# Contrast adjustment on one core: three of seven stores moved to ScalarE's queue, the last tile clipped and stored in halves

## The chip, the core and the metric

The kernel runs on one core of one Trainium2 chip. The metric is the device time of one execution in microseconds (us); before the change the median of three runs is 239.53 us (239.49 to 239.54). The core has five instruction streams that matter here: PE (TensorE), DVE (VectorE), ACT (ScalarE), POOL (GpSimd) and SP (SyncE). Each runs its own instructions in order. Transfers between device memory and the on-chip memory (128 partitions) are issued by one of these streams and then moved by the core's 16 DMA engines.

## What is computed

The input is a batch of 16 images with 3 planes of 512 x 512 float32 numbers, 50.33 MB. Each plane's contrast is stretched about its own mean, and the result is clipped to 0..1:

```python
def reference(x, factor):                      # x: 16 x 3 x 512 x 512, factor = 1.5
    mean = np.mean(x, axis=(2, 3), keepdims=True)
    return np.clip(mean + factor * (x - mean), 0, 1).astype(np.float32)
```

In other words out = clip(factor * x + (1 - factor) * mean, 0, 1). A plane's mean has to be known before any of its numbers can be written, so each number is loaded once, kept on chip, and stored once: 50.33 MB in and 50.33 MB out.

## The kernel before

A plane's 262144 numbers are cut into 16 rows of 16384, one row per partition. So one tile of 128 partitions x 16384 columns (8.39 MB) holds eight planes, and the 48 planes make six tiles, numbered 0 to 5. On chip there is one buffer named `ring` with three slots (BUFS = 3); tile t lies in slot t % 3. Tiles 3, 4 and 5 can be loaded only when the stores of tiles 0, 1 and 2 have left their slots. Slots, columns and waits are worked out by the framework from what each instruction reads and writes; the order of the instructions on each stream is the order in which the program is written (manual_schedule).

The steps of one tile:

- The load (line 77), issued by SP. Tile 0 comes in three pieces: columns 0 to 2047, 2048 to 8191, and 8192 to 16383. The others come in one.
- The row sums (function `add`). DVE sums the first 4352 columns (line 85), ACT the other 12032 with a copy onto themselves that also accumulates (line 89). For tile 0 this is done once for each half of the columns, with 4352 and 3840.
- The shift. PE multiplies the row sums by a block matrix whose entries are (1 - factor)/262144 inside each plane's 16 partitions (line 100), which leaves (1 - factor) * mean on each partition, in `bias`.
- The clip, two passes of DVE in place: multiply and add (line 103), then max with 0 and min with 1 (line 106). For tile 0 it is done in two column parts, 2048 and 14336 columns wide; here their stores are called 0a and 0b.
- The store (line 80), issued by SP, one for each part that is clipped.

The order in which SP issues is: the three pieces of load 0, loads 1 and 2, stores 0a, 0b, 1 and 2, loads 3, 4 and 5, stores 3, 4 and 5. So SP issues load 3 only after it has issued store 2, and that waits for the clip of tile 2. ACT issues no transfers. DVE's order is, tile after tile, its sum and then the two passes of the clip.

Of the kernel before, what the change touches and what calls it, by code (L numbers as in the profile page):

```python
# [1 line left out]

# [4 lines left out]


P = 128  # L10
ROW = 16384
HALF = ROW // 2
BUFS = 3
SHORT = 2048
SUM = 4352


@with_exitstack
def kernel(
    ctx: ExitStack,  # L20
    tc: tile.TileContext,
    x: bass.AP,
    factor: float,
    out: bass.AP,
):

    nc = tc.nc
    f32 = mybir.dt.float32  # L30
    Alu = mybir.AluOpType
    Act = mybir.ActivationFunctionType

    B, C, H, W = x.shape
    n_img, n_pix = B * C, H * W
    ppi = n_pix // ROW
    per_tile = P // ppi
    n_tiles = n_img // per_tile
    assert ppi * ROW == n_pix and per_tile * n_tiles == n_img

    factor = float(factor)
    wconst = (1.0 - factor) / float(n_pix)

    x_f = x.rearrange("b c h w -> (b c h w)")
    out_f = out.rearrange("b c h w -> (b c h w)")

    def dram(ap, t, c0=0, c1=ROW):
        return bass.AP(tensor=ap.tensor, offset=t * P * ROW + c0, ap=[[ROW, P], [1, c1 - c0]])

    consts = ctx.enter_context(tc.tile_pool(name="consts", bufs=1))  # L50
    xpool = ctx.enter_context(tc.tile_pool(name="xpool", bufs=1))
    small = ctx.enter_context(tc.tile_pool(name="small", bufs=1))
    psum = ctx.enter_context(tc.tile_pool(name="psum", bufs=1, space=bass.MemoryType.PSUM))


    sums = small.tile([P, 4 * n_tiles], f32, name="sums")
    bias = psum.tile([P, n_tiles], f32, name="bias")

    blockw = consts.tile([P, P], f32, name="blockw")
    blocks = blockw.rearrange("p (a b) -> p a b", b=ppi)  # L60
    nc.gpsimd.memset(blockw, wconst)  # L61
    for base, step in ((0, -ppi), (ppi - 1, ppi)):
        nc.gpsimd.affine_select(  # L63
            out=blocks,
            in_=blocks,
            compare_op=Alu.is_ge,
            fill=0.0,
            base=base,
            pattern=[[step, per_tile], [0, ppi]],
            channel_multiplier=1 if step < 0 else -1,  # L70
        )


    ring = xpool.tile([P, BUFS, ROW], f32, name="ring")

    def load(t, c0=0, c1=ROW):
        nc.sync.dma_start(out=ring[:, t % BUFS, c0:c1], in_=dram(x_f, t, c0, c1))  # L77

    def store(t, c0=0, c1=ROW):
        nc.sync.dma_start(out=dram(out_f, t, c0, c1), in_=ring[:, t % BUFS, c0:c1])  # L80

    def add(t, col, c0, c1, c2):
        xt = ring[:, t % BUFS, :]
        own = sums[:, 4 * t + col : 4 * t + col + 2]
        nc.vector.tensor_reduce(  # L85
            out=own[:, 0:1], in_=xt[:, c0:c1], axis=mybir.AxisListType.X, op=Alu.add
        )
        part = xt[:, c1:c2]
        nc.scalar.activation(out=part, in_=part, func=Act.Copy, accum_out=own[:, 1:2])  # L89
        return [own[:, 1:2], own[:, 0:1]]  # L90

    def compute(t, *cuts):
        xt = ring[:, t % BUFS, :]
        if t == 0:
            parts = add(t, 0, 0, SUM, HALF) + add(t, 2, HALF, HALF + SUM, ROW)
        else:
            parts = add(t, 0, 0, SUM, ROW)
        shift = bias[:, t : t + 1]
        for k, part in enumerate(parts):
            nc.tensor.matmul(shift, blockw, part, start=k == 0, stop=k == len(parts) - 1)  # L100
        for c0, c1 in zip((0, *cuts), (*cuts, ROW)):
            part = xt[:, c0:c1]
            nc.vector.tensor_scalar(  # L103
                out=part, in0=part, scalar1=factor, scalar2=shift, op0=Alu.mult, op1=Alu.add
            )
            nc.vector.tensor_scalar(  # L106
                out=part, in0=part, scalar1=0.0, scalar2=1.0, op0=Alu.max, op1=Alu.min
            )
            store(t, c0, c1)

    with tc.manual_schedule():
        load(0, 0, SHORT)
        load(0, SHORT, HALF)
        load(0, HALF, ROW)
        load(1)
        load(2)
        compute(0, SHORT)
        compute(1)
        compute(2)
        load(3)  # L120
        load(4)
        load(5)
        compute(3)
        compute(4)
        compute(5)


# [1 line left out]
_INS = ['x', 'factor']  # L129
_OUTS = [((16, 3, 512, 512), 'float32')]  # L130

_NUMBERS = {'factor': 1.5}


# [26 lines left out]
```

## Time and profile before

| what | value |
|---|---|
| median of three runs | 239.53 us |
| span of the profiled execution, first to last instruction | 237.3 us |
| moved by DMA | 100.66 MB, mean 424 GB/s over the span |
| DVE busy | 137.4 us, 58% of the span |
| ACT busy | 59.9 us, 25% |
| PE busy | 7.9 us, 3% |
| one clip pass of a whole tile (line 103, line 106) | 8.76 us, 8.70 us |
| ACT's sum of 12032 columns | 10.23 us |
| DVE's sum of 4352 columns | 4.68 us |

The profile is of one execution whose span is given; the time measured for a run is longer than the span by what lies before the first and behind the last instruction (2.2 us, taken against the median of the runs; the profiled execution's own total isn't given apart from its span). All times in the views count from the first instruction. A line such as "L103 DVE" is what line 103 of the kernel let DVE do. "SPq" is the instruction with which SP issues a transfer, and its time isn't that of the transfer. Where rows are merged ("x4"), the time runs from the first one's start to the last one's end. In brackets stands how long the engine was idle before, and what ended that. Rates in short stretches count a packet where it starts, so they jump by whole packets.

### The profile page before, as it was taken

The numbers are of one execution on the slowest core, as the hardware profiler recorded it, in microseconds if no ns is written. First come the engines' busy times: TensorE is split into PE (matmuls) and PEld (weight loads), VectorE is DVE, ScalarE is ACT, GpSimd is POOL, SyncE is SP. The second block draws the span as 40 slices with busy tenths as digits, with TensorE's granted clock in tenths as the row PEclk, the third lists the DMA queues.
The fourth block names the chain that finished last, engine by engine and source line by source line (L and its number), as shares of the span: only waits on it lengthen the run. The fifth ranks groups of instructions, "written<-read, shape, count | busy, mean of one in ns | idle before, by whom it ended". The sixth has DMA issues, their size and how long they took to land.

```text
span 237.3 us, 186 instructions
## 1 busy us (share of the span) xinstructions
PE 7.9 (3%) x28; PEld 6.9 (3%) x28; DVE 137.4 (58%) x21; ACT 59.9 (25%) x15; POOL 1.1 (0%) x7
## 2 busy tenths in 40 slices
PE   0010100010001000000000000100000000000000
PEld 0010100010001000000000000100000000000000
DVE  0071899949998998000000043499989998991000
ACT  2051300980492000000000049319509800000000
POOL 1000000000000000000000000000000000000000
DMA  7999989899799798989899998989899998989894
GB/s 289 418 442 442 530 353 530 353 486 398 331 464 454 341 530 353 530 353 519 365 442 442 398 486 353 530 354 530 353 475 409 431 453 376 508 353 530 353 530 177
DMA packets 2160, 100.66 MB, mean 424 GB/s; under 512 B 240, under 2 KB 240, under 8 KB 240
## 3 DMA queue, kind: packets, MB, share of 16 engines
q1 hardware_dynamic: 2160, 100.66, 98.7%
HBM read 50.33 MB, written 50.33 MB: 424 GB/s over the span
## 4 chain that ended last, share of the span: by engine, by line
DVE 43%; DMA 36%; ACT 9%; PE 2%; SPq 1%; issue 0%; DVEq 0%; ACTq 0%
DMA ring<-in_x_dram 36%; DVE ring L103 18%; DVE ring L106 18%; ACT ring L89 9%; DVE sums L85 6%; PE bias L100 2%; SPq L77 1%; SPq L80 0%; DVEq L103 0%; ACTq L89 0%
## 5 line engine op out<-in xcount | busy, mean ns | idle before, releaser
L89 ACT ACTIVATE ring<-ring 128x12032 f32<-128x12032 f32 (+1 forms) x7 | 58.0, 8280 | 128.2 <-DMA ring<-in_x_dram 128.2
L85 DVE TENSOR_REDUCE sums<-ring 128x1 f32<-128x4352 f32 x7 | 32.8, 4683 | 63.9 <-DMA ring<-in_x_dram 63.9
L103 DVE TENSOR_SCALAR ring<-ring,bias 128x16384 f32<-128x16384 f32 (+2 forms) x7 | 52.8, 7538 | 12.9 <-PE bias L100 12.9
L106 DVE TENSOR_SCALAR ring<-ring 128x16384 f32<-128x16384 f32 (+2 forms) x7 | 52.3, 7476 | 0.2
L100 PE MATMUL bias<-sums,blockw 128*128 128x1 f32 x28 | 7.9, 360 | 189.1 <-ACT ring L89 175.4
L100 PEld LDWEIGHTS bias<-sums,blockw 128*128 128x128 f32 x28 | 6.9, 314 | 190.0 <-ACT ring L89 159.4
L89 ACT ACT_TABLE_LOAD x1 | 1.3, 1283 | 0.8 <-PEq L142 0.8
L89 ACT ACTIVATION_READ_ACCUMULATOR ring<-ring 128x1 f32 x7 | 1.3, 187 | 0.0
L63 POOL TENSOR_SCALAR_AFFINE_SELECT blockw<-blockw 128x128 f32<-128x128 f32 x2 | 0.7, 340 | 0.1
L61 POOL MEMSET blockw<- 128x128 f32 x1 | 0.2, 204 | 0.3 <-POOLq L142 0.3
L142 POOL MEMSET const-bfloat16-1.0<- 128x1 bf16 x1 | 0.1, 102 | 0.0
L142 POOL MEMSET const-uint8-127<- 128x1 uint8 x1 | 0.1, 102 | 0.0
L142 POOL MEMSET const-float32-0.0<- 128x1 f32 x1 | 0.1, 98 | 0.3 <-issue 0.3
L142 POOL MEMSET const-float32-1.0<- 128x1 f32 x1 | 0.1, 98 | 0.0
## 6 DMA issues: line engine op xcount, KB each, us to landing
out_dram<-ring SPq DMA_DIRECT2D x1, 7168.0 KB, 35.9
ring<-in_x_dram SPq DMA_DIRECT2D x1, 4096.0 KB, 20.8
ring<-in_x_dram SPq DMA_DIRECT2D x1, 3072.0 KB, 11.6
ring<-in_x_dram SPq DMA_DIRECT2D x1, 1024.0 KB, 4.7
out_dram<-ring SPq DMA_DIRECT2D x1, 1024.0 KB, 34.3
ring<-in_x_dram SPq DMA_DIRECT2D x5, 57.7
out_dram<-ring SPq DMA_DIRECT2D x5, 27.0
```

What stands on the lines that cost most here:

```text
L61: nc.gpsimd.memset(blockw, wconst)
L63: nc.gpsimd.affine_select(out=blocks, in_=blocks, compare_op=Alu.is_ge, fill=0.0, base=base, pattern=[[step, per_tile], [0, ppi]], channel ...
L77: nc.sync.dma_start(out=ring[:, t % BUFS, c0:c1], in_=dram(x_f, t, c0, c1))
L85: nc.vector.tensor_reduce(out=own[:, 0:1], in_=xt[:, c0:c1], axis=mybir.AxisListType.X, op=Alu.add)
L89: nc.scalar.activation(out=part, in_=part, func=Act.Copy, accum_out=own[:, 1:2])
L100: nc.tensor.matmul(shift, blockw, part, start=k == 0, stop=k == len(parts) - 1)
L103: nc.vector.tensor_scalar(out=part, in0=part, scalar1=factor, scalar2=shift, op0=Alu.mult, op1=Alu.add)
L106: nc.vector.tensor_scalar(out=part, in0=part, scalar1=0.0, scalar2=1.0, op0=Alu.max, op1=Alu.min)
L142: nc = _bacc.Bacc("TRN2", target_bir_lowering=False, num_devices=1)
```

## The change

Stores of tiles whose slot is 0, that is 0 and 3, are issued by ACT instead of SP; the others stay on SP. `compute` is split in two functions, `total` (the row sums) and `clip` (matmuls, the two passes, and the store), called in the same order as before for the first five tiles. Three things differ besides. The store of tile 3 is not issued from its clip but after the row sums of tile 4 have been put down, so on ACT it stands behind the sum of tile 4 and ahead of the sum of tile 5. On ACT the stores 0a and 0b stand behind the two sums of tile 0 and ahead of the sum of tile 1. And tile 5 is clipped in two halves of 8192 columns, each stored on its own (here 5a and 5b).

```diff
     def store(t, c0=0, c1=ROW):
-        nc.sync.dma_start(out=dram(out_f, t, c0, c1), in_=ring[:, t % BUFS, c0:c1])
+        queue = nc.scalar if t % BUFS == 0 else nc.sync
+        queue.dma_start(out=dram(out_f, t, c0, c1), in_=ring[:, t % BUFS, c0:c1])
...
-    def compute(t, *cuts):
+    parts = {}
+
+    def total(t):
+        if t == 0:
+            parts[t] = add(t, 0, 0, SUM, HALF) + add(t, 2, HALF, HALF + SUM, ROW)
+        else:
+            parts[t] = add(t, 0, 0, SUM, ROW)
+
+    def clip(t, *cuts):
         xt = ring[:, t % BUFS, :]
...
-            store(t, c0, c1)
+            if t != BUFS:
+                store(t, c0, c1)
...
-        compute(0, SHORT)
-        compute(1)
-        compute(2)
+        total(0)
+        clip(0, SHORT)
+        total(1)
+        clip(1)
+        total(2)
+        clip(2)
         load(3)
         load(4)
         load(5)
-        compute(3)
-        compute(4)
-        compute(5)
+        total(3)
+        clip(3)
+        total(4)
+        store(3)
+        clip(4)
+        total(5)
+        clip(5, HALF)
```

On SP's queue this leaves: loads 0 (three pieces), 1 and 2, stores 1 and 2, loads 3, 4 and 5, stores 4, 5a and 5b.

More of the change, by code (lines that the diff above doesn't have):

```diff
@@ L90, in add @@
         return [own[:, 1:2], own[:, 0:1]]
-    def compute(t, *cuts):
+    parts = {}
[5 more added lines that the diff above has]
+    def clip(t, *cuts):
         xt = ring[:, t % BUFS, :]
[L94 to L97, printed above, removed]
         shift = bias[:, t : t + 1]
-        for k, part in enumerate(parts):
-            nc.tensor.matmul(shift, blockw, part, start=k == 0, stop=k == len(parts) - 1)
+        for k, part in enumerate(parts[t]):
+            nc.tensor.matmul(shift, blockw, part, start=k == 0, stop=k == len(parts[t]) - 1)
         for c0, c1 in zip((0, *cuts), (*cuts, ROW)):
```

## The prediction

> **What bounds the kernel now.** I read the page's DMA rows first, then the chain of waits, then a table of stretches cut where one transfer follows another, and last the timeline of each engine.
>
> ```profile
> DMA packets 2160, 100.66 MB, mean 424 GB/s; under 512 B 240, under 2 KB 240, under 8 KB 240
> q1 hardware_dynamic: 2160, 100.66, 98.7%
> DVE 43%; DMA 36%; ACT 9%; PE 2%; SPq 1%; issue 0%; DVEq 0%; ACTq 0%
> ```
>
> One queue kept the 16 DMA engines busy for 98.7% of the span. The chain names DVE for 43%, but it follows whatever released a transfer last; the next table says that the transfers themselves leave no room. Its columns: stretch, length, busy time of the engines, granted clock, DMA share, GB/s.
>
> ```profile
> 0.80:1.80 1.00, 0.00 (x0) 0.00 (x0) 0.00 (x0) 1.00 (x1) 0.86 (x3) 1.00 0.00 0
> ...
> 57.90:60.30 2.40, 0.00 (x0) 0.00 (x0) 2.40 (x1) 0.00 (x0) 0.00 (x0) 1.00 1.47 437
> 60.30:61.40 1.10, 0.00 (x0) 0.00 (x0) 1.10 (x1) 0.00 (x0) 0.00 (x0) 1.00 0.00 0
> ```
>
> The same table, one transfer a line:
>
> ```profile
> 41.50:62.00 20.50, 1.01 (x4) 0.93 (x4) 17.43 (x3) 10.32 (x2) 0.00 (x0) 1.00 0.90 367
> ...
> 81.40:100.70 19.30, 0.00 (x0) 0.00 (x0) 12.31 (x2) 0.00 (x0) 0.00 (x0) 1.00 0.99 431
> 100.70:120.10 19.40, 0.00 (x0) 0.00 (x0) 0.00 (x0) 0.00 (x0) 0.00 (x0) 1.00 1.01 436
> ...
> 178.10:197.50 19.40, 1.18 (x4) 1.00 (x4) 18.61 (x4) 10.32 (x2) 0.00 (x0) 1.00 1.01 439
> 197.50:216.80 19.30, 0.00 (x0) 0.00 (x0) 17.03 (x2) 0.00 (x0) 0.00 (x0) 1.00 1.00 435
> ```
>
> Whole tiles of 8.39 MB follow each other every 19.4 us, loads and stores alike. Only load 2 took 20.5: for 1.1 us after 60.3 no new row began. Twelve tiles at 19.36 make 232.3 us; with 1.1 for that stall, 1.2 at the end (no row after 236.1 of 237.3) and the 2.7 left over for the start (first issue at 0.80, no packet before 1.80, a slow first microsecond), that is the span. So nothing but the stall can be gained, and the question is whether the change leaves the DMA engines without work.
>
> The timeline: SP's issues of stores 0a to 2 merged, then tile 1's sum and clip and tile 2's sum.
>
> ```profile
> 30.52 63.63 SPq L80 DMA_DIRECT2D out_dram<-ring  x4
> 41.93 10.23 ACT L89 ACTIVATE ring<-ring 128x12032 f32<-128x12032 f32 x1 [15.86 <-DMA ring<-in_x_dram]
> 53.43 8.76 DVE L103 TENSOR_SCALAR ring<-ring,bias 128x16384 f32<-128x16384 f32 x1 [3.07 <-PE bias L100]
> 62.22 8.70 DVE L106 TENSOR_SCALAR ring<-ring 128x16384 f32<-128x16384 f32 x1
> 62.40 10.23 ACT L89 ACTIVATE ring<-ring 128x12032 f32<-128x12032 f32 x1 [10.15 <-DMA ring<-in_x_dram]
> ```
>
> The timeline again, SP alone: load 4.
>
> ```profile
> 101.08 0.34 SPq L77 DMA_DIRECT2D ring<-in_x_dram  x1
> ```
>
> ACT's starts give the landings of loads 1 and 2 (41.93, 62.40); load 4 is issued at 101.08, when store 1 has landed. A landing shows some 0.4 us after the slowest engine goes on to its next row, so the engines finish store 1 at 100.7. Store 2, issued at 93.82, is waiting there by then: a reserve of 100.7 - (93.82 + 1.0) = 5.9 us, with the 1.0 from issue to first packet at the start.
>
> The packet count gives the size of a piece: 15 transfers x 16 engines x 9 = 2160, eight partition rows and one small entry (the 240) per engine and transfer. A full row (64 KB) takes 19.4/8 = 2.42 us; a row of store 0a (2048 columns, 8 KB) 0.30; a row of store 0b (14336 columns) 2.12. Store 0a is 2.42 in all, store 0b 16.9.
>
> **The change part by part.** The profiled span of 237.3 lies 2.2 below the median of 239.53, which I add as a constant.
>
> 1. *Stores 0a and 0b on ACT.* Now both stand in SP's queue behind loads 1 and 2 and move nothing before 61.4. On a second queue they can move from 31.5 (issue 30.52 + 1.0) and 46.8, and delay the loads by what they put between. The trace has one queue only, so how the engines share is unknown. Bounds for load 2's delay: none (rows stay behind the loads), or 2.42 + 16.5 = 18.9 (equal shares by bytes from 46.8 on, where load 2 has 16.5 of work left and store 0b 16.9). I take alternation row by row, because the packets of the trace are rows: bursts of one row on each of the 16 engines every 2.42 us. Load 1's rows change at 22.2 + 2.42k (load 0 landed at 22.58, less 0.4), so the first 8 KB row goes in at 31.9, after its row 4; one follows each load row, and the eighth comes after row 3 of load 2. Store 0b, long issued, then goes in after rows 4 to 7: four rows, or three if the engine had already taken its next row at 31.9. Load 2 is delayed by 2.42 + 4 x 2.12 = 10.9 and lands at 73.3 (71.2 with three).
>
> 2. *ACT's order.* The issue of 0b waits for the second clip pass of tile 0 (45.76), and ACT's sum of tile 1 is queued behind it: it starts at 46.2 instead of 41.93 (load 1 lands at 43.2 to 44.4, so that is hidden in the same wait). From the start of ACT's sum to the clip is 53.43 - 41.93 = 11.50; both passes take 8.77 + 0.02 + 8.70 = 17.49. Clip 1 ends at 75.2 instead of 70.9 and store 1 can move at 76.2; the engines have loads and store 0 until 81.4, which hides it with 5.2 to spare. DVE's sum of tile 2 follows until 79.9.
>
> 3. *Store 2 and what stands behind it.* ACT's sum of tile 2 starts at 73.3, its clip at 84.8 (DVE is free at 79.9, and 0.7 for the matmuls makes 80.6, so ACT ends last), store 2 is issued at 84.8 + 17.49 + 0.07 = 102.4 and moves at 103.4. SP is in order: loads 3, 4 and 5 are behind that issue, although their slots are free (store 0 done before 90, store 1 at 101.1). The engines run dry at 100.7: **a gap of 2.7 us**, passed on whole to everything later, since the rest is back to back. With three rows it is 0.6. The point from which it costs anything is load 2 landing at 100.7 - 1.0 - 29.1 = 70.6.
>
> 4. *Restart and mixing.* After a gap the first rows are slow: the first microsecond of data at the start moved at 213 GB/s against 418 in the next, half a microsecond lost; a store needn't repeat it, so 0 to 0.5, taken as 0. Switching between load and store rows: load 5, followed by a store, landed 178.57 - 159.21 = 19.36 after load 4, no loss; load 2, followed by the small rows of 0a, lost 1.1. So for each of some 15 switches between nothing and 1.1, at most 8 of them with small rows (+8.8), and at best the old stall goes (-1.1). I take no change.
>
> 5. *Store 3 on ACT, issued after ACT's sum of tile 4.* Times of before, to be shifted by the gap: that sum ends at 169.5, clip 3 at 168.9, so ACT doesn't wait, and the issue (0.34) is over long before load 5 lands. Store 3 moves from 170.6 beside load 5, which has three rows left; alternation (or equal bytes) delays load 5 by 7.3, to 185.9. ACT's sum, then clip 5 at 185.9 + 11.5 = 197.4, against 197.08 now, where DVE ends last: 0.3 later. The total of work is unchanged, and store 4 (191.8) is there before store 3 is through at 197.5. Nothing on the path; if the store went wholly first, load 5 would land at 197.9, and the first half of store 5 would move at 219.4 against 216.8, a gap of 2.6.
>
> 6. *The last tile in halves.* Passes of 8192 columns by the line through the rows for 2048 and 14336 (1.29 and 7.69; 1.23 and 7.63): 4.49 + 4.43 = 8.92 a half, 17.84 for both, 0.4 more than now. Half 5a is issued near 206.4, half 5b near 215.3; 5a's 9.7 us of rows cover 5b behind store 4's end at 216.8. Store 5 is already there at 214.64 + 1.0, so the earlier start gains nothing. Rows half as long cost nothing that load 0c (4 MB: 22.55 - 12.86 = 9.7) doesn't show.
>
> 7. *Issues.* SP has three fewer and one more, ACT three more, 0.34 each, all beside waits. POOL and PE are untouched.
>
> Sum: 2.7 + 0 + 0 = +2.7, so 239.5 + 2.7 = **242.2**; this case alone runs from 239.0 (three rows, the stall gone: 0.6 - 1.1) to 243.3 (a slow restart and a little mixing).
>
> The Trainium skill, DMA: Bandwidth & Descriptors, section Queues, rings and completion order, says that an engine goes round its queues by packets and drains one of about 9 to 17 descriptors before it switches. If the nine entries of a transfer on an engine are one such packet, the second rival below holds and the sum would be 0; no run here shows yet which unit it is.
>
> **The rivals.** *Equal shares by bytes.* Store 0a takes its 1 MB at half rate by 36.3, 0b and load 2 end nearly together: load 2 lands at 62.4 + 18.9 = 81.3, store 2 is issued at 110.4, and the gap is 10.7 (9.6 net if the stall goes): 249.1 to 250.2. For it: equal competitors. Against: the trace moves whole rows one after another on an engine.
>
> *Whole transfers in turn* (or one order for both queues). Load 2 lands no later than 62.4 + 2.4 = 64.9, tile 2's clip waits for DVE (80.6), store 2 is issued at 98.1 and moves at 99.1, before 100.7. No gap: 239.5; the placement on two queues then does nothing. This is also where it ends on the other side: if 0a's small rows no longer stand behind load 2's last row and that 1.1 us stall goes with them, 238.4. It decides as long as load 2 lands by 70.6. For it: nine entries a transfer. Against: nothing in the trace marks the nine as one unit.
>
> *Stores first, or costly mixing.* Priority of stores gives 10.7 and the 2.6 of step 5: 252.8; mixing at 1.1 on each of eight small rows adds up to 8.8 to the sum: 251.
>
> **How the numbers follow.** Rows in turn 0.52, equal bytes 0.20, whole transfers 0.18, stores first or costly mixing 0.10. A change under 0.2% (0.48 us) can't be told from none here. Slower: 0.46 of the first, all of the second and the last: 0.76. Same: 0.04 + 0.12 = 0.16. Faster: 0.02 + 0.06 = 0.08. The range reaches from 238.6 to 250.2, leaving out the lucky end of whole transfers and most of the last case.
>
> **What would show it.** Two queues in the DMA rows; ACT's sum of tile 1 at 46.2 and of tile 2 at 71 to 73 (65: whole transfers; 80 or more: equal bytes); SP issuing store 2 at 100 to 102 and loads right behind it; a hole in GB/s just after 100; later tiles shifted by the same few microseconds; no hole after 200. It is wrong if load 2 lands before 70.6, or if rows of 64 KB take clearly over 2.42 us while both queues move.

## The result and the profile after

The changed kernel takes 243.37 us (243.29 to 244.03) against 239.51 (239.11 to 239.54) beside it: 1.0167 times the time, 95% interval 1.0155 to 1.0179, or 3.9 us slower. The forecast was 242.2 in a range of 238.6 to 250.2. The profiled execution took 243.29 with a span of 241.5, so 1.8 us lie around the span; spans compared, the change cost 4.2.

The page of the changed kernel, its DMA rows:

```profile
DMA packets 2304, 100.66 MB, mean 417 GB/s; under 512 B 256, under 2 KB 256, under 8 KB 256
q1 hardware_dynamic: 1872, 83.89, 81.6%
q10 hardware_dynamic: 432, 16.78, 16.1%
```

There are two queues now, and together they fill 97.7% of the engines' span where one filled 98.7%. The bytes are the same; the time that the engines were without work, or slow, has grown. The table of stretches shows where (columns as before: stretch, length, engines, clock, DMA share, GB/s):

```profile
81.20:100.50 19.30, 1.01 (x4) 0.93 (x4) 15.92 (x2) 2.17 (x2) 0.00 (x0) 1.00 0.97 422
100.50:102.90 2.40, 0.00 (x0) 0.00 (x0) 1.53 (x1) 0.00 (x0) 0.00 (x0) 1.00 0.00 0
102.90:119.90 17.00, 0.00 (x0) 0.00 (x0) 0.00 (x0) 0.00 (x0) 0.00 (x0) 1.00 1.00 432
```

From 100.5 to 102.9 no row was moved: a hole of 2.4 us, counted from the last engine's end to the first one's start (2.6 on the mean of the 16 engines). What it waited for stands in the timeline; these are the lines of ACT and DVE on tiles 1 and 2 and of SP behind them:

```profile
46.14 10.23 ACT L90 ACTIVATE ring<-ring 128x12032 f32<-128x12032 f32 x1 [20.16 <-DVE ring L111]
73.05 10.23 ACT L90 ACTIVATE ring<-ring 128x12032 f32<-128x12032 f32 x1 [16.58 <-DMA ring<-in_x_dram]
84.54 8.76 DVE L108 TENSOR_SCALAR ring<-ring,bias 128x16384 f32<-128x16384 f32 x1 [4.82 <-PE bias L105]
102.09 0.34 SPq L81 DMA_DIRECT2D out_dram<-ring  x1
102.61 21.60 SPq L77 DMA_DIRECT2D ring<-in_x_dram  x3
```

In the kernel before, the clip of tile 2 and the issue of store 2 are these lines:

```profile
76.26 8.76 DVE L103 TENSOR_SCALAR ring<-ring,bias 128x16384 f32<-128x16384 f32 x1 [0.75 <-PE bias L100]
93.82 0.33 SPq L80 DMA_DIRECT2D out_dram<-ring  x1
```

ACT's sum of tile 1 started at 46.14, let go by DVE and no longer by the load, since the issue of store 0b stands ahead of it. Load 2 landed at 73.05 instead of 62.40, the clip of tile 2 started at 84.54 instead of 76.26, and SP issued store 2 at 102.09 instead of 93.82. Only then came load 3, although nothing else held it.

The hole isn't all. DVE's sum of tile 3 and ACT's sum of tile 4 start at 143.25 and 162.66, later by 3.5 than before (139.79 and 159.21), and the span ends 4.2 later. The missing parts are longer stretches in which no row was started, at two places where loads and stores meet. The same table, first of the changed kernel (store 2's last row, and the row of load 5 before store 3 comes in):

```profile
120.10:122.85 2.75, 0.00 (x0) 0.00 (x0) 0.00 (x0) 0.00 (x0) 0.00 (x0) 1.00 0.00 0
174.25:176.85 2.60, 0.00 (x0) 0.00 (x0) 2.56 (x1) 0.00 (x0) 0.00 (x0) 1.00 0.00 0
```

and of the kernel before, just behind the end of its store 2, and in load 5's last row:

```profile
120.10:121.80 1.70, 0.00 (x0) 0.00 (x0) 0.00 (x0) 0.00 (x0) 0.00 (x0) 1.00 0.00 0
175.65:177.45 1.80, 0.00 (x0) 0.00 (x0) 1.80 (x1) 0.00 (x0) 0.00 (x0) 1.00 0.00 0
```

A row takes 2.42 us. In the kernel before the engines start theirs over some 0.6, so 1.7 to 1.8 us without a start is the rhythm of undisturbed engines. In the changed kernel they start within 0.15 and 0.35 of each other at these places, which would leave 2.3 and 2.1; 2.75 and 2.6 is more. The packets of the trace settle it: averaged over the 16 engines, the row at 120 lasted 0.73 too long and the one at 174 0.81, where the kernel before has 0.0 and 0.1. I call these pauses.

Load 2's delay can be read in the trace too. Two stretches of the changed kernel, with the packets and MB of each queue (q1 is SP's, q10 ACT's); first 42.8 to 53.7 us, load 2's first four rows beside store 0a:

```profile
q1 hardware_dynamic: 71, 4.19, 88.8%
q10 hardware_dynamic: 64, 0.52, 11.3%
```

4.19 MB are 64 full rows, 0.52 MB are 64 rows of 8 KB: each of 16 engines took four of each in turn, and the queues' bytes stand eight to one. (The 7 others on q1 are completion entries, the small entries at a transfer's end.) And 68.6 to 72.7 us, the end of load 2 beside store 0b, with the rates in 40 slices of 0.1 us:

```profile
GB/s 0 0 0 0 0 0 0 0 0 0 0 0 0 0 0 0 1119 3357 1678 2797 0 0 0 0 0 0 0 0 0 0 0 0 0 0 0 0 559 559 3357 3916
q10 hardware_dynamic: 31, 1.78, 100.0%
q1 hardware_dynamic: 16, 0.00, 0.2%
```

SP's queue moves nothing more than 16 entries of a few bytes, one per engine: the completion entries of load 2. The packets show its last data row ending at 70.55 on the slowest engine. Ten of the entries follow by 70.64, but six engines reach theirs only at 72.4 to 72.7, behind one more row of store 0b. ACT sees the load at 73.05, 2.5 us after the last data row, where some 0.4 is usual.

### The profile page after: what moved, and what is told of

It is laid out like the page before. It is cut to its first block, busy times and chain, and to the rows that moved or that the text cites. A ratio compares the mean times of both kernels' runs of the same rounds, so it can differ in the third digit from the quotient of the medians.

```text
span 241.5 us, 188 instructions
## 1 busy us (share of the span) xinstructions
PE 7.5 (3%) x28; PEld 6.7 (3%) x28; DVE 137.7 (57%) x23; ACT 59.9 (25%) x15; POOL 1.1 (0%) x7
## 4 chain that ended last, share of the span: by engine, by line
DMA 25%; DVE 24%; ACT 21%; another core or an unknown queue 18%; PE 1%; issue 1%; SPq 1%; ACTq 0%; DVEq 0%
DMA ring<-in_x_dram 25%; ACT ring L90 21%; DVE ring L108 11%; DVE ring L111 11%; DVE sums L86 2%; PE bias L105 1%; SPq L77 0%; ACTq L81 0%; SPq L81 0%; ACTq L169 0%; DVEq L108 0%; ACTq L90 0%
## 5 line engine op out<-in xcount | busy, mean ns | idle before, releaser
L108 DVE TENSOR_SCALAR ring<-ring,bias 128x16384 f32<-128x16384 f32 (+3 forms) x8 | 53.0, 6622 | 22.3 <-PE bias L105 22.3
L111 DVE TENSOR_SCALAR ring<-ring 128x16384 f32<-128x16384 f32 (+3 forms) x8 | 52.5, 6560 | 0.3
```

The costliest lines, as they stand in the source:

```text
L108: nc.vector.tensor_scalar(out=part, in0=part, scalar1=factor, scalar2=shift, op0=Alu.mult, op1=Alu.add)
L111: nc.vector.tensor_scalar(out=part, in0=part, scalar1=0.0, scalar2=1.0, op0=Alu.max, op1=Alu.min)
```

## The experiments

The experiments set three theories against each other. A: load 2 is late, hence store 2, hence a hole; the two pauses come on top. B: two queues side by side cost engine time, in the head (loads 1 and 2) and in the tail (load 5). C: store 3 on ACT and the halves carry the loss. Each edit below is against the changed kernel, or, where the heading says so, against the kernel before. In brackets behind a time stand its ratio to the kernel before and the 95% interval of that ratio.

### Only stores 0a and 0b on ACT

```diff
-        queue = nc.scalar if t % BUFS == 0 else nc.sync
+        queue = nc.scalar if t == 0 else nc.sync
...
-            if t != BUFS:
-                store(t, c0, c1)
+            store(t, c0, c1)
...
-        store(3)
...
-        clip(5, HALF)
+        clip(5)
```

> Only stores 0a and 0b go to ACT's queue; store 3 is back on SP, issued from its clip, and tile 5 is clipped and stored whole. Theory A (load 2 is late, so store 2 is issued at 102.1 and the DMA engines are empty for 2.4 us; the rest of the +3.9 is two pauses of a row near 120 and 175 us): store 2 issued at 102.1 again, load 3 landing some 3.4 us later than before the change; 242.0 to 243.4, the lower end if the pause near 175 belongs to store 3 running beside load 5. Rival B (the two queues side by side cost engine time, the tail as much as the head): the tail's share goes, about 241.5. Rival C (store 3 and the halves carry the loss): 239.5.

243.83 us (1.0179, 1.0162 to 1.0196). Store 2 was issued at 102.2 and the tile 3 sum started at 143.32, as with the whole change. Both pauses are there (0.72 near 120, and 1.14 in load 5's last row, though store 3 now waits behind it on the same queue). So this part alone carries the whole loss. C falls, and so does what B gave to the tail. The time is 0.4 above the top of what A expected.

### Only the tail

```diff
-        queue = nc.scalar if t % BUFS == 0 else nc.sync
+        queue = nc.scalar if t == BUFS else nc.sync
```

> Only store 3 goes to ACT's queue, and tile 5 is clipped and stored in halves; stores 0a and 0b are back on SP. Theory A: no gap near 100 us, since store 2 is issued at 93.8; 239.5, or 240.3 if store 3 beside load 5 costs the 0.8 us by which the last landings fell further behind. Rival B: 241 to 242. Rival C: 243.4.

239.7 us (1.001, 1.0 to 1.0019). Store 3 ran beside load 5, which landed at 186.4 instead of 178.6, yet nothing came of it: the clip of tile 5 was in time, and the total of rows is the same. The row in which store 3 joins load 5 lasted 0.41 too long, against 0.1 in load 5's last row before, and little of that shows in the time. Two queues at once cost next to nothing here, and the halves bring nothing.

### Load 3 ahead of store 2

```diff
         clip(1)
+        load(3)
         total(2)
         clip(2)
-        load(3)
```

> As the changed kernel, but SP issues load 3 ahead of store 2, right behind store 1. Theory A: load 3 waits for store 0 alone (landed at 86.4), so the engines have its rows at 100.5 when store 1 ends, the hole near 100 us is gone, and store 2, issued at 102.1 as before, follows it: 243.4 - 2.4 = 241.0, and down to 239.5 if the pauses near 120 and 175 us go with the hole. Rival B (mixing): 243.4, since both queues are used as much. ACT's sums of tiles 1 and 2 start at 46.1 and 73.1 as in the changed kernel.

240.6 us (1.0038, 1.0026 to 1.0049). SP in the timeline of this kernel:

```profile
86.50 0.33 SPq L77 DMA_DIRECT2D ring<-in_x_dram  x1
102.10 0.34 SPq L81 DMA_DIRECT2D out_dram<-ring  x1
```

and the stretches around the former hole:

```profile
97.55:99.95 2.40, 0.00 (x0) 0.00 (x0) 2.40 (x1) 0.00 (x0) 0.00 (x0) 1.00 1.01 437
99.95:102.35 2.40, 0.00 (x0) 0.00 (x0) 2.08 (x1) 0.00 (x0) 0.00 (x0) 1.00 1.02 437
```

Store 2 is issued as late as before (102.10), but load 3 has been waiting since 86.5, the rate stays at 437 GB/s, and 2.8 of the 3.9 us are back. So the hole needed both a late store 2 and a load 3 that stands behind it in SP's order. What remains (1.1 in the median) the trace shows as pauses (0.44 near 119, 0.66 when store 3 joins load 5) and a second, short hole at 217: here load 5 landed only at 196.8, store 5a was issued at 217.30, and the engines, which ended store 4 from 217.2 on, waited 0.7 on average for its rows at 218.1.

### Store 0b in four pieces with short rows

```diff
-            if t != BUFS:
+            if t == 0 and c0:
+                for p0 in range(c0, c1, 3584):
+                    store(t, p0, p0 + 3584)
+            elif t != BUFS:
                 store(t, c0, c1)
```

> As the changed kernel, but store 0b is issued as four stores of 3584 columns (rows of 14 KB instead of 56 KB), one after the other on ACT. If the engines take one row of each queue in turn whatever its size, at most four rows of 0.53 us and eight of 0.30 stand ahead of load 2's last row, so load 2 lands at 66 to 67 instead of 73.05; ACT's sum of tile 1 starts 1 us later (three more issues), tile 2's clip then waits for DVE (near 81.5), store 2 is issued near 99.1 and moves before the engines are empty at 100.5: no hole, 239.5 to 241.0. If the queues share by bytes, load 2 lands at 73 or later and the time stays at 243.4.

241.9 us (1.0097, 1.0074 to 1.012). The timeline of this kernel:

```profile
68.50 10.23 ACT L90 ACTIVATE ring<-ring 128x12032 f32<-128x12032 f32 x1 [10.40 <-DMA ring<-in_x_dram]
99.65 0.34 SPq L81 DMA_DIRECT2D out_dram<-ring  x1
```

The same bytes in rows a quarter as long delayed load 2 to 68.50 and not 73.05: engines take turns by rows, not by bytes. That is still later than the 66 to 67 expected; the engines ended load 2's last row between 64.6 and 67.6, and the last one counts. The clip of tile 2 then waited for DVE, started at 82.10, and store 2 was issued at 99.65. Of the hole, 15 engines had 0.1 to 0.7 us left (0.4 on average) and the sixteenth, which was behind, had none. But the time is 0.9 above what was expected. The trace shows where it went: the two pauses (0.71 and 1.01) are as long as with the hole, and in the last 1.1 us of the transfers a single engine was still moving rows.

### A shorter sum of tile 2 on ACT

```diff
-            parts[t] = add(t, 0, 0, SUM, ROW)
+            parts[t] = add(t, 0, 0, 6400 if t == 2 else SUM, ROW)
```

> As the changed kernel, but tile 2's row sums are cut at 6400 columns for DVE instead of 4352, so that ACT's sum takes 9984 columns (8.49 us instead of 10.23). Theory A (the hole is the lateness of store 2): DVE's sum ends at 75.04 + 6.88 = 81.9, the clip starts near 82.7 instead of 84.5, store 2 is issued at 100.2 instead of 102.1, and the hole of 2.4 us shrinks by 1.9 to 0.5: 243.4 - 1.9 = 241.5. Rival B (the hole is something of the queues): stays at 243.4.

241.99 us (1.0098, 1.0082 to 1.0115), 1.4 less than the changed kernel. SP's issue of store 2 in this kernel:

```profile
100.73 0.34 SPq L81 DMA_DIRECT2D out_dram<-ring  x1
```

That is 1.36 earlier, and the time went down by the same. On the mean of the engines the hole is 1.4 us instead of 2.6, and the pauses are unchanged (0.75 and 0.78). So the time follows the issue of store 2 through the hole. (The sum took 8.53 us as expected, but load 2 landed 0.3 later this time, and with both engines ending near 82 the gain was smaller than the 1.9 that I had worked out.)

### The kernel before with tile 0 stored whole

```diff
-        compute(0, SHORT)
+        compute(0)
```

> The kernel before, all on SP, but tile 0 is clipped in one piece and stored once, so that rows of 64 KB and not of 8 KB stand behind load 2's last row. If the pause of 1.1 us in that row comes from the small rows, it goes: 238.4. If it comes from the change from loads to stores, or from the time of the run, it stays: 239.5.

239.56 us (0.9998, 0.9989 to 1.0008), and the pause in load 2's last row is still there (1.30 on average; 1.11 with the small rows). Small rows behind a load don't cause it.

### Load 3 early, and the tail as before

```diff
         clip(1)
+        load(3)
         total(2)
         clip(2)
-        load(3)
...
-        store(3)
...
-        clip(5, HALF)
+        clip(5)
```

(with `queue` and `store` as in the first experiment)

> Stores 0a and 0b on ACT and load 3 ahead of store 2 on SP, the tail as in the kernel before (store 3 on SP from its clip, tile 5 whole). With no hole near 100 us and no second queue in the tail: 239.5 to 240.6. If the pause near load 5's end depends on store 3 running beside load 5, it goes and the time is at the lower end; if it belongs to the change from loads to stores in whichever way, it stays at 240.6.

239.81 us (1.002, 1.0002 to 1.0039), runs from 239.2 to 241.5. At its best it equals the kernel before; it doesn't beat it. The profiled execution was the longest: its last 2.2 us are one engine alone. Its row at the end of load 5 lasted 0.2 too long on average, where the first experiment, with store 3 on SP in the same way, had 1.14; so whether store 3 beside load 5 matters for that pause isn't decided here.

### The kernel before, with store 2 made late

```diff
+            if t == 2:
+                nc.vector.tensor_scalar(
+                    out=part, in0=part, scalar1=0.0, scalar2=1.0, op0=Alu.max, op1=Alu.min
+                )
             store(t, c0, c1)
```

> The kernel before, all on SP, with one more pass of tile 2's max and min (8.70 us, the values don't change), so that store 2 is issued at 102.5 instead of 93.8 with a single queue. Theory A: store 1 still ends at 100.7, store 2's rows start near 103.4, a hole of 2.6 us: 242.2, and up to 243.2 if the pause of some 0.8 us at the end of store 2, seen in the changed kernel near 120 us, comes with it. Rival B (the loss is of two queues): 239.5, as SP alone waits longer.

244.04 us (1.0185, 1.0169 to 1.02), 0.8 above the top of what A expected; that had counted one pause, and the one in load 5 came as well. This is the disputed cost by itself, with one queue. SP in the timeline of this kernel, store 2 and the loads behind it:

```profile
102.62 0.33 SPq L80 DMA_DIRECT2D out_dram<-ring  x1
103.05 21.69 SPq L77 DMA_DIRECT2D ring<-in_x_dram  x3
```

The stretches, the last two lines being the hole and the quiet time at the end of store 2:

```profile
81.40:100.80 19.40, 0.00 (x0) 0.00 (x0) 19.33 (x3) 0.00 (x0) 0.00 (x0) 1.00 0.91 395
100.80:103.40 2.60, 0.00 (x0) 0.00 (x0) 1.75 (x1) 0.00 (x0) 0.00 (x0) 1.00 0.00 0
...
120.65:123.40 2.75, 0.00 (x0) 0.00 (x0) 0.00 (x0) 0.00 (x0) 0.00 (x0) 1.00 0.00 0
```

A hole of 2.6 us, and the pauses with it: 0.74 at the end of store 2 and 1.01 in load 5's last row, where the kernel before has 0.0 and 0.1. The loss (4.6 us, where the change has 3.9) is of the same make as that of the change, without a second queue. Nothing of the loss needs B.

### The same, late but in time

(the edit against the kernel of the experiment above)

```diff
+                head = part[:, 0:HALF]
                 nc.vector.tensor_scalar(
-                    out=part, in0=part, scalar1=0.0, scalar2=1.0, op0=Alu.max, op1=Alu.min
+                    out=head, in0=head, scalar1=0.0, scalar2=1.0, op0=Alu.max, op1=Alu.min
                 )
```

> As the kernel before with an extra max and min on tile 2, but on half of its columns (4.43 us), so that store 2 is issued at 98.3: later than before (93.8), yet its rows are ready at 99.1, ahead of 100.7 when store 1 ends. If only a hole costs, there is none: 239.5, the pauses near 120 and 180 us as small as in the kernel before (0.0 and 0.1). If those pauses come from how late load 3 is put behind store 2, and not from the hole, they appear (0.8 and 1.0): 241.2. If lateness costs its own length, 239.5 + 4.4 = 244.

240.58 us (1.0039, 1.0012 to 1.0065), ten runs from 239.2 to 242.0. SP's issue of store 2 in this kernel:

```profile
98.28 0.33 SPq L80 DMA_DIRECT2D out_dram<-ring  x1
```

That is 4.5 later than before; the profiled execution took 239.2 with no hole, and pauses of 0.0 and 0.1 as in the kernel before. So 4.5 us of lateness can be free. But five of the ten runs took 241 to 242: none of the expectations has such a spread.

### The same kernel profiled twice more, and a quarter of the pass

The first two are single executions of the kernel of the experiment above, unchanged. The third is a kernel with `0 : HALF // 2` in place of `0:HALF`.

> The same kernel as the one with half an extra pass, for another profile: its times lay between 239.2 and 242.0, and the profiled execution was the shortest, without pauses near 120 and 180 us. A longer execution should show where its time lies: if at those two places, pauses of 0.7 to 1.1 us each with no hole near 100 us (then the hole isn't needed for them); if near 100 us, a hole of up to 2 us in some executions.

239.22 us, without the two pauses (0.0 and 0.1).

> As the look before it, a third profile of the same kernel: 239.2 without pauses, or 240 to 242 with them.

241.33 us, an execution of the longer kind. There is no hole near 100, and the average pause is small (0.07 and 0.19), but one engine lost 0.9 and 0.8 us in the two rows about the end of store 2 (117 to 124 us) and about another 1 in load 5's last row, and moved the last rows alone: 15 engines were through at 236.6, it at 238.4.

> The kernel before with the extra max and min on 4096 columns of tile 2 (2.2 us): store 2 issued at 96.1, load 3 right behind it, 3.6 us ahead of the last moment (99.7) instead of 1.4. If what lengthens some executions is a small reserve, 239.5 to 239.9; if it is any delay of store 2 or the longer work on DVE, 240.5 as with half a pass.

239.39 us (1.0006, 0.9995 to 1.0016), one run of ten at 240.4, the others at or below 239.7. With some 3.5 us of reserve the time is as before; with 1.4 some executions are longer. The profiled execution (239.71) still had 0.45 in load 5's last row.

## Why the prediction was right, point by point

**The bound** held. Whatever won time back did so by keeping the engines supplied, and no version was measurably faster than the kernel before.

**Step 1, the two queues.** Rows in turn, the likeliest case, is what the trace shows, and load 2 landed at 73.05 where the sum had 73.3. The number was right by luck: I had four rows of 0b ahead of load 2's last row. The engines had already taken load 1's row 5 when store 0a came, so the first small row went in at 34.0 and not at 31.9, and on the six engines that ended load 2 there were three rows of 0b, as in my variant for an engine that has already taken its next row (two on the other ten). The fourth stood ahead of the completion entry, which takes its turn like a row. The Trainium skill, DMA: Bandwidth & Descriptors, section Queues, rings and completion order, has turns by packets of about 9 to 17 descriptors; if the nine entries of a transfer were such a unit, load 2 would have landed by 64.9. Here the unit is one entry: 64 rows of each queue in the same 10.9 us.

**Step 2, ACT's order**: 46.14 (46.2 forecast), store 1 issued at 75.22 (75.2 for the end of its clip), and covered.

**Step 3, the hole**: store 2 at 102.09 (102.4), the hole 2.4 (2.7). That the issue of store 2 sets it, and SP's order passes it on, is shown by three runs: load 3 ahead removes it, a shorter sum shrinks it by about what the issue gains, and the kernel before gets it when its store 2 is late.

**Step 4, restart and mixing**, is the term that was mis-sized: taken as 0. Up to the hole it does come out at 0, but because two amounts cancel, which is luck. The rows of load 1 that met store 0a lost 0.5 in all (31 to 42 us, by the rows that lasted too long) and those of load 2 that met 0b lost 0.6 (54 to 61 us), while the 1.1 in load 2's last row, which the kernel before has, is gone; so the engines end store 1 at 100.5 where they ended it at 100.7. The restart cost 0.1 (the first row after the hole took 2.50). What I had missed is that pauses come with the hole: 0.7 near 120 and 0.8 near 174, so that a hole of 2.4 goes with a loss of 3.9, where the sum had 2.7. Bounds of -1.1 to +8.8 held them, but for another reason than mine: they come with one queue too, and without small rows.

One of the two signs of being wrong was there in part. While both queues moved, rows of 64 KB took 2.42 between 42.8 and 53.7, but 2.46 to 2.64 on average in three rows of load 1 and 2.55 and 2.91 in two of load 2. The turns by rows held all the same; these tenths are the mixing of step 4.

**Step 5 and 6, the tail**: load 5 landed 7.8 later in the tail-only kernel (7.3 forecast), and store 3 on ACT and the halves were worth nothing, as summed (239.7). **Step 7** had nothing on the path.

Around the span lie 1.8 us and not 2.2: the median of 239.53 was set beside a span of 237.3 that belonged to a shorter execution.

**What stays open** is the cause of the pauses. Shown: they lie in rows where loads and stores meet, or one row beside; they don't need small rows or two queues; load 2's last row has one of 1.1 to 1.5 us in every kernel whose store 0 waits behind it; after a hole of 1.4 us or more near 100 us the two later changes have them on all engines (0.7 to 1.1 on average), and without one they run from nothing, or one engine alone, to 0.7. They are as long after the hole of 1.4 as after that of 2.6, and the kernel with short rows had them with a hole of 0.4, so the hole's length isn't what counts. One thought is that a hole lets the engines start again in step: they started the first row after it within 0.15 us of each other in the changed kernel, and within some 0.6 elsewhere. The kernel with short rows speaks for it. Fifteen of its engines started at 100.5 within 0.12 of each other, and all fifteen lost 0.5 to 1.1 in the row at 117.5; the sixteenth started that row 1.6 later and took 2.42. But 0.45 was lost in load 5's last row by engines that started it over 0.7 us (the quarter pass), and no experiment varied the starts alone. So it isn't shown.

## What to carry to other kernels

A store put beside a load still running was paid by the load here, row for row, and the row's length in bytes set the price; ask what waits for that load, and whether the store was needed earlier at all. In a kernel that the DMA engines bound, look for the moment at which each queue would run dry, and for what the issuing engine holds back behind a wait: here a load with a free slot stood behind a store that was not ready. A few us of reserve there are worth keeping: a hole of 2.4 us cost 3.9 here, one of 2.6 cost 4.6, and with a reserve of 1.4 some executions were still longer.

## What was not expected of the hardware

- Entries of two queues are taken in turn, one row each, whatever the size: 64 rows of 64 KB and 64 of 8 KB in 10.9 us in the changed kernel.
- The completion entry of a load takes its turn as well: with rows of 56 KB beside it, load 2 was reported 2.5 us after its last data row, 2.1 later than usual.
- The last row before loads and stores change places can last 0.7 to 1.5 us longer than 2.42 on average (1.1 in load 2's last row before the change, 0.73 and 0.81 in the changed kernel), or about 1 on one engine alone; the cause is open.
- A store that found the engines empty had its first row going 0.84 us after the issue (102.09 to 102.93), less than the 1.0 taken from the first load.
